# Even mixer of the second block: the convolution's norm ahead of the third pair of heads, its spread in an accumulator bank, and the modulation steps dealt out at other places

## The chip, the cores and the metric

The kernel runs on one core of a Trainium2 chip. The metric is device time in microseconds of one execution. A core has five engines that work from their own instruction streams in order: TensorE (PE, matmuls; its weight loads are PEld), VectorE (DVE), ScalarE (ACT), GpSimd (POOL) and SyncE (SP, which here only issues transfers).

## The reference, cut to what matters

Three transformer blocks follow one another on one sequence of 256 tokens with 1024 channels, in fp32. The change lies in the second block, in the mixer of its first layer:

```python
def even_mixer(hm, w_in, q_g, k_g, conv_w, conv_b, ln_g, ln_b, w_out, rope, kv_prefix):
    proj = hm @ w_in
    q = rms_norm_2(proj[..., :ATTN_WIDTH]..., q_g)         # 8 heads of 64
    k, v = split_kv(proj[..., ...], k_g)                   # 2 kv heads
    q = apply_rope(q, *rope); k = apply_rope(k, *rope)
    k = concatenate([kv_prefix[0], k]); v = ...            # 256 context rows ahead
    attn = block_attention(q, k, v)
    g = u * sigmoid(gate)                                  # 512 channels each
    g = depthwise_conv(g, conv_w) + conv_b                 # 31 taps
    g = silu(layer_norm(g, ln_g, ln_b))
    return concatenate([attn, g]) @ w_out

def second_block(...):
    for i in range(2):
        m = ada_mod(c, ada_w[i], ada_b[i])                 # silu(c) @ w + b, 6 x 1024 numbers
        hn = modulate(rms_norm_2(h, norm1_g[i]), m[0], m[1])
        ...                                                # i = 0: the context with ada_mod(c_ctx), then even_mixer
        h = h + m[2] * mixer(hn)                           # i = 1: short_conv_mixer
        h = h + m[5] * ec_moe(modulate(rms_norm_2(h, norm2_g[i]), m[3], m[4]), ...)
```

`ec_moe` has 16 experts, each of which takes its 32 best tokens; 12 MB of weights belong to each expert. The modulation matrices `ada_w` hold 24 MB for each layer.

## The kernel before

**The mixer's stages.** `even_mixer` (L1107) norms the block's input, projects k and v (`ev_kv`), the queries (`ev_q`), and value and gate of the convolution's first two channel groups (`gated(0)`, `gated(1)`). Then it norms the 256 context rows (transposes `nt` L525; squares' sums, `newton` L357 to L367, `across` L379, which spreads a column of scales over all partitions by a matmul with ones; L563 scales, L571 casts), projects the context's k and v, and takes norm and rotary embedding of the heads (L581 to L1236, with transposes `tr` L598). From there on the source calls `convolve` of four channel groups, `gated(2)`, `gated(3)`, and `attend` of four pairs of heads, and the layer norm over the convolution's channels (L1252 to L1274). Last comes the output projection `ev_out` in `residual` (4 weight slabs, the convolution's half of the channels first), then the router, the choice of tokens, their gathering, and the experts' matmuls (L1387).

**Steps within these.** `gated(g)` (L1142) projects two slabs, gates them (L1154), writes the result to DRAM (`evd`, L1158) and reads it back four times shifted (`sh`, L1162), all on SP. `convolve` is 32 matmuls of 32x256 (L1178). `attend` scores each pair of heads in four matmuls (`fsc`, L651), takes maxima on DVE (L655), exponentials on ACT (L658), reciprocals and products on DVE (L660, L663), transposes on PE (`fpt`, L666), copies on ACT and multiplies with v (`ev_o`, L671). In the norm of the convolution `ev_mean` is L1254, `ev_var` L1264; the spread (L1265, by `across` L386) takes a PSUM bank of `gen`.

**Weights.** A slab of 128x2048 (1 MB) comes by SP into one of the 7 places of the ring `w` (`slab`, L338). `weights` (L400) loads it (L406) and splits each half of it into a rounded part (ACT, L392) and the rest (DVE, L393) in one of three `ws` buffers; `mm3` then has three matmuls (L424 to L426). The modulation's slabs go through the same ring (L1001).

**Modulation.** `Ada.steps` (L985) is a generator. One step is one chunk of 512 outputs: two slabs. Even chunks run on PE: 16 matmuls (L1007), a copy on ACT (L1028), two transposes (L1030). Odd chunks (listed in `VEC`) run on ACT (L1013) and DVE (7 accumulations `ada_acc`, L1015), with four column matmuls at the end (`ada_t`, L1023). In `even_mixer` 14 steps are left, which `k.step(n)` deals out: `weights` asks for .46 of a step after each slab, `gated(g)` for `PACE[1][g]`, the place behind the context's k and v for `PACE[1][4]`, and `k.step(99)` for what is left. So a call of `k.step` sets where in the program the step's loads and instructions stand.

**PSUM.** Banks are `acc` (3), `o` (1) and `gen` (4, taken in turn by scores, transposes, modulation and small results).

**What sets the order.** No order is written by hand. A list scheduler takes the program's order as priority and a time model of its own, and fixes each engine's order of instructions when the program is built; the engines then run their lists in order. A wait in such a list holds all that stands behind it on that engine.

**The experts' weights.** `place` (L1378) asks for expert slabs early, in 21 places (the ring's seven, seven of `more`, the others where buffers come free), and the loads stand in SP's list among the others.

Of the kernel before, what the change touches and what calls it, by code (L numbers as in the profile page):

```python
# [250 lines left out]
HOLD = 8  # L251

FIRST = 10
VEC, PACE = [[1,3,5,7,9,11],[1,3,5,7,9,11]], (.46, (2,2,3,2,4))

RAW = 3

# [27 lines left out]
class Kern:  # L285
# [27 lines left out]
    def t(self, name):  # L313
        return self.tab[name]
# [58 lines left out]
        self.nc.vector.tensor_scalar(x, ss, 1.0 / dim, EPS, op0=OP.mult, op1=OP.add)  # L373
        return self.newton(x, n, pool)

    def across(self, col, pool, name):

        n = col.shape[-1]
        if pool is None:  # L379
            d = self.sm.tile([128, 512], F32, tag="sq", name=name, bufs=1)[:, :128 * n].rearrange("p (n s) -> p n s", n=n)  # L380
        else:
            d = pool.tile([128, n, 128], F32, name=name, bufs=1)
        self.nc.vector.tensor_tensor(d, self.ident[:, None, :].to_broadcast([128, n, 128]),
                                     col[:, :, None].to_broadcast([128, n, 128]), op=OP.mult)
        p = self.gen(name)
        self.spread = self.nc.tensor.matmul(p[:, :128 * n], self.ones, d.rearrange("p n s -> p (n s)"), start=True, stop=True)  # L386
        return p[:, :128 * n]

# [677 lines left out]
def block2(k, ada, ns):  # L1066
    nc, tc = k.nc, k.tc
    with ExitStack() as cx:
        pl = cx.enter_context(tc.tile_pool(name="b2", bufs=1))
        ring = cx.enter_context(tc.tile_pool(name="ring2", bufs=RING_B))  # L1070
        k.rings.append((ring, RING_B))
        k.load_table("t2", pl)
        more = cx.enter_context(tc.tile_pool(name="more", bufs=MORE))
        for l in range(2):
            if l == 0:
                ns, route = even_mixer(k, ada, ns, pl, more)
            else:
                n = len(k.loads)
                ns, route = short_conv(k, ada, ns, pl, srow, last)
            if l == 0:  # L1080
                box = []

                def start(room):
                    gain, shift = ada.gains(1, "norm11", 0)
                    box.append(k.norm_state(gain=gain, shift=shift, fp=Cut([(room[0], 0)], 2), n=4))
                    return lambda c: k.norm_part(box[1], k.x, c, 256)

                def early():
                    box.append(pl.tile([128, D], F32, tag="mrow", name="sc_mrow"))
                    ada.row(1, 2, box[0])  # L1090
                last = moe(k, ada, l, ns, route, pl, more, start, early, None)
                srow, ns = box
            else:
                fin = FinalNorm(k, pl)
                moe(k, ada, l, ns, route, pl, more, fin.start, fin.load, k.loads[n + HOLD])
        k.rings.pop()
        return fin.finish()
# [24 lines left out]
def even_mixer(k, ada, ns, bp, more):  # L1122
    nc, tc, t = k.nc, k.tc, k.t
    with ExitStack() as cx:
# [20 lines left out]
        def gated(g):  # L1145
            box = []

            def evac(i, p):
                if i == 0:
                    box.append(p)  # L1150
                    return
                h = gpool.tile([128, S], name="evh")
                nc.scalar.activation(h, p, AF.Tanh, scale=0.5)
                nc.vector.scalar_tensor_tensor(gp[:, g, 15:15 + S], h, 1.0, box[0], op0=OP.add, op1=OP.mult)  # L1154
            k.columns("ev_ug", g, xs, 8, evac)
            k.step(PACE[1][g])
            d = tc.dram_tile([128, S + 32], F32, name=f"evd{g}")
            nc.sync.dma_start(d, gp[:, g])  # L1158
            sh = shs[g % 2]
            for b in range(4):  # L1160
                src = bass.AP(tensor=d.tensor, offset=d.offset + b, ap=[[S + 32, 32], [32 * (S + 32), 4], [1, S + 28]])
                nc.sync.dma_start(sh[32 * b:32 * b + 32], src)  # L1162
            return sh
# [3 lines left out]
        def diagonals(g):  # L1167
            dg = dgs[g] = dgp.tile([128, 4, 8, 32], name="dg")
            for c in range(4):
                nc.gpsimd.tensor_tensor(dg[:, c], t("ev_half")[:, None, :].to_broadcast([128, 8, 32]),  # L1170
                                        cw[:, 4 * g + c, :, None].to_broadcast([128, 8, 32]), op=OP.mult)

        def convolve(g, sh):
            dg = dgs[g]
            p = k.acc("ev_conv")
            for j in range(8):
                for c in range(4):
                    nc.tensor.matmul(p[32 * c:32 * c + 32, :S], dg[:, c, j], sh[:, c, 4 * j:4 * j + S], start=j == 0, stop=j == 7,  # L1178
                                     tile_position=(0, 32 * c))
            nc.scalar.activation(cv[:, g], p[:, :S], AF.Identity, bias=t("ev_cb")[:, g:g + 1])  # L1180

        def attend(j):
            o = k.bank("o", "ev_o")
            k.full_attention(atp, o[:, :S], qt[:, j], kt_, lambda i, h: v[:, i, 64 * h:64 * h + 64], 4)
            k.split(yh[:, j], yl[:, j], o[:, :S])
# [14 lines left out]
        sh = [gated(0), gated(1)]  # L1200
# [37 lines left out]
        at = cx.enter_context(tc.tile_pool(name="evat", bufs=1))  # L1238
# [1 line left out]
        convolve(0, sh[0])  # L1240
        diagonals(2)
        sh.append(gated(2))
        attend(0)
        convolve(1, sh[1])
        diagonals(3)
        sh.append(gated(3))
        attend(1)
        convolve(2, sh[2])
        attend(2)
        convolve(3, sh[3])  # L1250

        mean = k.acc("ev_mean")  # L1252
        for g in range(4):
# [7 lines left out]
        var = k.acc("ev_var")  # L1261
        for tt in range(2):
            for g in range(4):
                nc.tensor.matmul(var[:, tt:tt + 1], sq[g // 2][:, g % 2, 128 * tt:128 * tt + 128], k.ones[:, 0:1], start=g == 0, stop=g == 3)  # L1264
        rs = k.across(k.rsqrt(var[:, 0:2], 2, 512), at, "ndiag2")  # L1265
        for g in range(4):
            f = sqp.tile([128, 2, S], F32, tag="nf", name="ev_y")
            y, h = f[:, 0], f[:, 1]
            nc.vector.scalar_tensor_tensor(y, cv[:, g], t("ev_lng")[:, g:g + 1], rs, op0=OP.mult, op1=OP.mult)
            nc.vector.tensor_scalar(y, y, t("ev_lnb")[:, g:g + 1], None, op0=OP.add)  # L1270
            nc.scalar.activation(h, y, AF.Tanh, scale=0.5)
            nc.vector.scalar_tensor_tensor(y, h, 1.0, y, op0=OP.add, op1=OP.mult)
            k.split(yh[:, 4 + g], yl[:, 4 + g], y, 0.5)
        attend(3)  # L1274
        k.step(99)
        return k.residual("ev_out", (yh, yl), 8, mrow, sqp, route.half, order=(1, 0)), route
# [755 lines left out]
```

## Time and profile before

| | |
|---|---|
| median of 3 runs | 2212.45 us (2212.28 to 2213.82) |
| profiled execution | 2207.99 us, of which the span is 2206.2 us |
| PE busy | 1827.9 us (83%) |
| DVE, ACT busy | 1056.3 us (48%), 723.5 us (33%) |
| mean granted TensorE clock | 0.889 |
| bytes by DMA | 638.00 MB, 289 GB/s over the span |
| instructions | 35790 |

The profile divides the span into slices, engines and waits. Busy time of PE is modelled: an instruction that runs at the lower clock is longer in it, and a busy PE is not PE at its peak. The profile shows each fp32 matmul of these sizes as two rows (16 matmuls of L1007 are 32 rows; a transpose is one). The granted clock is a share of full speed. Of the whole span, the DMA engines move 417 to 419 GB/s in the stretches of the experts and 96 to 400 in the others.

### The profile page before, as it was taken

What the parts mean: (1) busy time and instruction counts of PE and PEld (TensorE: products, weight loads), DVE (VectorE), ACT (ScalarE), POOL (GpSimd) and SP (SyncE); (2) the same over time, 40 slices, a digit from 0 to 9 for tenths busy, and PEclk for the clock granted to TensorE, in tenths of its full rate; (3) what the DMA queues carried; (4) which work ended last, traced back from release to release, by engine and by line L of the source; (5) the groups of instructions that cost most, each with busy time, mean ns of one, the idle gap of its engine ahead of it and who ended that gap; (6) DMA issues with size and microseconds to landing.
All of it is one profiled execution on the core that took longest, in us unless ns stands there. A gap on an engine that the chain in (4) does not pass through costs nothing.

```text
span 2206.2 us, 35790 instructions
## 1 busy us (share of the span) xinstructions
PE 1827.9 (83%) x14836; PEld 1283.5 (58%) x14836; DVE 1056.3 (48%) x2343; ACT 723.5 (33%) x1363; POOL 47.6 (2%) x90
## 2 busy tenths in 40 slices
PE   7989989898666666789867666667989999999999
PEld 5777877555322222269632222224768998988997
DVE  4885787754100000157500000004877985778984
ACT  4454544342000000035300000003654664555763
POOL 1000010001000000000100000000100000000000
PEclk9999999988877787799987777778999999999999
DMA  9654679938999999997799999999623454434553
GB/s 270 234 198 165 231 298 331 367 132 325 418 419 419 418 418 419 418 416 278 275 418 418 418 419 418 418 419 369 191 96 115 172 192 154 132 136 153 180 177 122
DMA packets 100594, 638.00 MB, mean 289 GB/s; under 512 B 11294, under 2 KB 14238, under 8 KB 28496
## 3 DMA queue, kind: packets, MB, share of 16 engines
q1 hardware_dynamic: 97632, 627.03, 72.7%
q0 software_dynamic: 1360, 4.49, 1.2%
q10 hardware_dynamic: 1440, 4.21, 0.5%
q8 instruction: 116, 1.90, 0.3%
q14 instruction: 46, 0.38, 0.0%
HBM read 632.96 MB, written 2.72 MB: 288 GB/s over the span
## 4 chain that ended last, share of the span: by engine, by line
PE 51%; DMA 38%; DVE 7%; ACT 2%; issue 1%; SPq 0%; ACTq 0%
DMA w<-in_moe_w_down 6%; DMA w<-in_moe_w_up 6%; DMA more<-in_moe_w_up 5%; DMA more<-in_moe_w_down 5%; DMA w<-in_moe_w_gate 4%; PE up L426 4%; PE up L425 3%; PE up L424 3%; DMA more<-in_moe_w_gate 3%; DMA own<-in_moe_w_up 2%; DMA own<-in_moe_w_down 2%; DMA own<-in_moe_w_gate 2%; PE down L425 2%; PE down L426 2%; PE down L424 2%; DVE ws L393 2%
## 5 line engine op out<-in xcount | busy, mean ns | idle before, releaser
L393 DVE TENSOR_TENSOR ws<-w,ws 128x1024 fp32r<-128x1024 f32 (+5 forms) x316 | 376.9, 1195 | 171.6 <-ACT ws L392 169.4
L392 ACT CAST ws<-w 128x1024 fp32r<-128x1024 f32 (+5 forms) x316 | 320.6, 1020 | 271.7 <-PE down L426 63.9
L1486 ACT ACTIVATE hd<-gu 128x256 f32<-128x256 f32 x32 | 12.3, 383 | 717.0 <-PE gu L1387 717.0
L1487 DVE SCALAR_TENSOR_TENSOR hd<-hd,gu 128x256 f32<-128x256 f32 x32 | 13.5, 421 | 479.8 <-ACT hd L1486 479.8
L1387 PE MATMUL gu<-w,xst 128*32 128x256 f32 x1376 | 122.0, 483 | 62.0 <-DMA w<-in_moe_w_gate 34.3
L425 PE MATMUL up<-ff_xh,ws 128*128 128x256 f32 x608 | 171.1, 284 | 2.6 <-DVE ws L393 2.6
L426 PE MATMUL up<-ff_xl,ws 128*128 128x256 f32 x608 | 170.4, 283 | 2.7 <-DVE ff_xl L393 2.7
L424 PE MATMUL up<-ff_xh,ws 128*128 128x256 f32 x608 | 168.2, 283 | 0.1
L1387 PE MATMUL gu<-more,xst 128*32 128x256 f32 x1344 | 111.0, 457 | 65.7 <-DMA more<-in_moe_w_up 43.5
L1387 PEld LDWEIGHTS gu<-w,xst 128*32 128x32 f32 x1376 | 44.0, 130 | 135.0 <-DMA w<-in_moe_w_up 53.8
L1501 DVE SCALAR_TENSOR_TENSOR ysm<-dn,gcol,moe_mq 128x256 f32<-128x256 f32 x30 | 14.5, 484 | 221.0 <-PE dn L1387 221.0
L1387 PEld LDWEIGHTS gu<-more,xst 128*32 128x32 f32 x1344 | 43.2, 125 | 128.9 <-DMA more<-in_moe_w_up 68.8
L425 PEld LDWEIGHTS up<-ff_xh,ws 128*128 128x128 f32 x608 | 115.7, 190 | 3.7 <-DVE ws L393 3.5
L426 PEld LDWEIGHTS up<-ff_xl,ws 128*128 128x128 f32 x608 | 115.3, 190 | 3.1 <-DVE ff_xl L393 3.1
L424 PEld LDWEIGHTS up<-ff_xh,ws 128*128 128x128 f32 x608 | 114.0, 190 | 0.5 <-ACT ff_xh L392 0.5
L1387 PE MATMUL gu<-ws,xst 128*32 128x256 f32 x608 | 56.4, 498 | 24.3 <-DMA ws<-in_moe_w_up 14.1
L1015 DVE SCALAR_TENSOR_TENSOR ada_acc<-w,ada_st,ada_acc 128x512 f32<-128x512 f32 x98 | 73.6, 758 | 4.7 <-ACT ada_acc L1013 4.2
L424 PE MATMUL down<-ws,ff_h 128*128 128x512 f32 x176 | 69.7, 396 | 0.0
L425 PE MATMUL down<-ws,ff_l 128*128 128x512 f32 x176 | 69.5, 395 | 0.0
L1387 PE MATMUL dn<-w,ht 128*32 128x256 f32 x672 | 55.4, 465 | 14.6 <-DMA w<-in_moe_w_down 8.3
L1387 PE MATMUL dn<-more,ht 128*32 128x256 f32 x672 | 55.4, 474 | 12.6 <-DMA more<-in_moe_w_down 8.3
L426 PE MATMUL down<-ws,ff_h 128*128 128x512 f32 x176 | 63.8, 396 | 0.0
(650 smaller groups left out, 4032.5 us busy)
## 6 DMA issues: line engine op xcount, KB each, us to landing
w<-in_wd SPq DMA_DIRECT2D x144, 1024.0 KB, 5.0
w<-in_ada_w SPq DMA_DIRECT2D x48, 1024.0 KB, 5.5
more<-in_moe_w_up SPq DMA_DIRECT2D x48, 1024.0 KB, 19.8
w<-in_moe_w_gate SPq DMA_DIRECT2D x48, 1024.0 KB, 14.1
w<-in_moe_w_down SPq DMA_DIRECT2D x46, 1024.0 KB, 14.3
more<-in_moe_w_down SPq DMA_DIRECT2D x46, 1024.0 KB, 19.9
w<-in_moe_w_up SPq DMA_DIRECT2D x38, 1024.0 KB, 19.9
more<-in_moe_w_gate SPq DMA_DIRECT2D x36, 1024.0 KB, 19.9
```

The source lines that it names most:

```text
L392: self.nc.scalar.copy(hi, src)
L393: self.nc.vector.tensor_tensor(lo, src, hi.bitcast(F32), op=OP.subtract)
L424: mm(out, lh, rh, start=first, stop=False)
L425: mm(out, ll, rh, start=False, stop=False)
L426: mm(out, lh, rl, start=False, stop=last)
L1015: nc.vector.scalar_tensor_tensor(acc[v], w[:, kt], s, acc[v], op0=OP.mult, op1=OP.add)
L1387: nc.tensor.matmul(out[32 * c:32 * c + 32], lhs(kt), w(1024 * kk + 256 * c, 256), start=kt == 0, stop=kt == 7, tile_position=(0, 32 * c))
L1486: nc.scalar.activation(hd, gu[:, 0:256], AF.Tanh, scale=0.5)
L1487: nc.vector.scalar_tensor_tensor(hd, hd, 1.0, gu[:, 0:256], op0=OP.add, op1=OP.mult)
L1501: nc.vector.scalar_tensor_tensor(y, dn[:, :256], gcol[:, e:e + 1], mq, op0=OP.mult, op1=OP.mult)
```

## The change

Two numbers lists and the order of calls in `even_mixer` are changed. `PACE[1]`, the steps that `gated(0)` to `gated(3)` and the place behind the context's k and v ask for, goes from (2,2,3,2,4) to (1,1,1,1,3). `k.step(2)` is called in three new places: behind `convolve(2)`, behind `convolve(3)` and behind `attend(2)`; all 14 steps are dealt when the second of them is done, so the third call and `k.step(99)` find none. `attend(0)` goes behind `gated(3)`, the whole norm of the convolution ahead of `attend(2)`. The norm's spread takes a bank of `acc`.

```diff
-VEC, PACE = [[1,3,5,7,9,11],[1,3,5,7,9,11]], (.46, (2,2,3,2,4))
+VEC, PACE = [[1,3,5,7,9,11],[1,3,5,7,9,11]], (.46, (1,1,1,1,3))
...
-    def across(self, col, pool, name):
+    def across(self, col, pool, name, wide=False):
...
-        p = self.gen(name)
+        p = (self.acc if wide else self.gen)(name)
...
         convolve(0, sh[0])
         diagonals(2)
         sh.append(gated(2))
-        attend(0)
         convolve(1, sh[1])
         diagonals(3)
         sh.append(gated(3))
+        attend(0)
+        convolve(2, sh[2])
+        k.step(2)
         attend(1)
-        convolve(2, sh[2])
-        attend(2)
         convolve(3, sh[3])
+        k.step(2)
 
         mean = k.acc("ev_mean")
...
-        rs = k.across(k.rsqrt(var[:, 0:2], 2, 512), at, "ndiag2")
+        rs = k.across(k.rsqrt(var[:, 0:2], 2, 512), at, "ndiag2", True)
...
             k.split(yh[:, 4 + g], yl[:, 4 + g], y, 0.5)
+        attend(2)
+        k.step(2)
         attend(3)
         k.step(99)
```

Lines from the norm's mean on stand one later in the changed file, from the router on three later.

**PE, from the context's norm to its projection.** `nt` are the transposes of the context rows, `ndiag` the spread of its scales, `ada` and `ada_t` modulation. Before:

```order
L1023 MATMUL ada_t<-ones,ada_acc 128x1 x4
L1337 MATMUL rshift<-wg,ones 128x16 x8
L525 MATMUL nt<-t_70,ev_w 128x128 x16
L1007 MATMUL ada<-w,ada_st 32x256 x16
L1030 MATMUL ada_t<-t_70,ada_ms 128x128 x2
L1023 MATMUL ada_t<-ones,ada_acc 128x1 x4
L386 MATMUL ndiag<-ev_w,ones 128x256
```

After:

```order
L525 MATMUL nt<-t_70,ev_w 128x128 x11
L386 MATMUL ndiag<-ev_w,ones 128x256
L1007 MATMUL ada<-w,ada_st 32x256 x16
L1023 MATMUL ada_t<-ones,ada_acc 128x1 x4
```

The spread stands ahead of the modulation that stood ahead of it, one group of `ada_t` columns is gone from here, and the shifts of the router and five of the transposes stand earlier, among the projections.

**PE, from the last transposes of the queries (`tr`) to the first scores (`fsc`).** `ev_conv` is the convolution. Before:

```order
L598 MATMUL tr<-t_70,ev_w 128x128 x10
L1007 MATMUL ada<-w,ada_st 32x256 x16
L1023 MATMUL ada_t<-ones,ada_acc 128x1 x4
L1007 MATMUL ada<-w,ada_st 32x256 x12
L1030 MATMUL ada_t<-t_70,ada_ms 128x128 x2
L1007 MATMUL ada<-w,ada_st 32x256 x4
L1178 MATMUL ev_conv<-ev_w 32x256 x16
L651 MATMUL fsc<-ev_w 128x512
```

After:

```order
L1007 MATMUL ada<-w,ada_st 32x256 x16
L598 MATMUL tr<-t_70,ev_w 128x128 x8
L1023 MATMUL ada_t<-ones,ada_acc 128x1 x4
L1030 MATMUL ada_t<-t_70,ada_ms 128x128 x2
L651 MATMUL fsc<-ev_w 128x512 x2
```

One modulation step and 16 matmuls of the convolution stand behind the first scores instead of ahead of them, and another step stands ahead of the transposes. Up to the first scores of the program's list, 176 of the 192 matmuls of L1007 stood in it before and 144 now; of L1023 48 of 56 and now 40; of the convolution's 80 and now 64.

**PE, from the scores of the last pairs to the first matmuls of `ev_out`.** Before:

```order
L666 MATMUL fpt<-t_70,ev_w 128x128 x8
L386 MATMUL ndiag_4602<-ndiag_4600,ones 128x256
L671 MATMUL ev_o<-ev_w 64x256
L651 MATMUL fsc<-ev_w 128x512 x2
L671 MATMUL ev_o<-ev_w 64x256 x7
L666 MATMUL fpt<-t_70,ev_w 128x128 x4
L424 MATMUL ev_out_4721<-ws,ev_yh 128x512
```

After:

```order
L386 MATMUL ndiag_4482<-ndiag_4480,ones 128x256
L1023 MATMUL ada_t<-ones,ada_acc 128x1 x4
L666 MATMUL fpt<-t_70,ev_w 128x128 x4
L671 MATMUL ev_o<-ev_w 64x256
L651 MATMUL fsc<-ev_w 128x512
L666 MATMUL fpt<-t_70,ev_w 128x128 x4
L1007 MATMUL ada<-w,ada_st 32x256 x16
L671 MATMUL ev_o<-ev_w 64x256 x7
L424 MATMUL ev_out_4721<-ws,ev_yh 128x512
```

The first `ev_out` matmul stands behind 15 of the 16 score matmuls before, behind 13 now, and the last modulation step on PE stands right ahead of it.

**SP, from the last read of `sh` to the slabs of `ev_out` (`in_wd`).** Before:

```order
L1162 DMA sh<-evd_4341 32x4x284 x4
L1001 DMA w<-in_ada_w 128x2048
L1378 DMA more<-in_moe_w_up 128x2048
L1001 DMA w<-in_ada_w 128x2048
L406 DMA w<-in_wd 128x2048 x2
```

After:

```order
L1162 DMA sh<-evd_4125 32x4x284 x4
L1001 DMA w<-in_ada_w 128x2048
L1381 DMA more<-in_moe_w_up 128x2048
L1001 DMA w<-in_ada_w 128x2048
L1381 DMA more<-in_moe_w_up 128x2048
L1001 DMA w<-in_ada_w 128x2048 x4
L1381 DMA more<-in_moe_w_up 128x2048
L1001 DMA w<-in_ada_w 128x2048
L406 DMA w<-in_wd 128x2048 x3
```

Behind the last `sh` two modulation slabs and one expert slab were ahead of the first slab of `ev_out`; seven and three are now. The places that the slabs of `ev_out` take are those of steps 11 (PE), 12 (DVE) and 13 (PE) in both kernels. Ahead of the write of the third group's `evd` six modulation slabs stand in a row in the new list, two in the old.

## Rows read from the trace of the kernel before

**Rows 1.** Windows: start:end length, busy PE PEld DVE ACT POOL, clock, DMA share, GB/s.

```profile
316.00:355.60 39.60, 39.60 (x277) 30.54 (x275) 26.73 (x47) 17.59 (x29) 0.40 (x1) 0.98 0.77 295
368.00:405.30 37.30, 32.04 (x318) 24.59 (x318) 35.09 (x95) 12.13 (x23) 6.43 (x9) 0.95 0.95 322
415.00:440.00 25.00, 23.92 (x208) 13.16 (x208) 17.77 (x37) 12.62 (x28) 0.00 (x0) 1.00 1.02 407
440.00:457.00 17.00, 14.04 (x34) 6.37 (x36) 8.24 (x29) 5.65 (x14) 0.00 (x0) 0.51 0.52 213
457.00:471.50 14.50, 12.18 (x55) 6.24 (x52) 8.41 (x23) 6.84 (x20) 0.00 (x0) 0.87 0.00 0
471.50:500.20 28.70, 28.70 (x138) 21.63 (x137) 15.63 (x30) 12.32 (x24) 0.00 (x0) 1.00 0.52 202
530.00:1010.00 480.00, 335.85 (x3706) 163.93 (x3705) 75.48 (x158) 44.58 (x102) 0.80 (x14) 0.81 1.01 417
```

**Rows 2.** Timeline (start, length), PE: last of ev_out and first expert matmul.

```profile
499.94 0.40 PE L426 MATMUL ev_out<-ws,ev_yh 128*128 128x512 f32 x1
...
525.30 1.07 PE L1387 MATMUL gu<-w,xst 128*32 128x256 f32 x16
```

**Rows 3.** Timeline of SP there: the last early place and the loads behind.

```profile
519.75 0.33 SPq L1378 DMA_DIRECT2D x<-in_moe_w_down  x1
526.43 9.76 SPq L1378 DMA_DIRECT2D w<-in_moe_w_down  x6
```

**Rows 4.** Timeline of PE from the context's transposes to its projection.

```profile
356.01 1.94 PE L1337 MATMUL rshift<-wg,ones 128*128 128x16 f32 x16
357.80 3.00 PE L525 MATMUL nt<-t,ev_w 128*128 128x128 f32 x16
360.74 2.49 PE L1007 MATMUL ada<-w,ada_st 128*32 128x256 f32 x32
363.78 0.44 PE L1030 MATMUL ada_t<-t,ada_ms 128*128 128x128 f32 x2 [0.56 <-ACT ada_ms L1028]
364.35 1.02 PE L1023 MATMUL ada_t<-ones,ada_acc 128*128 128x1 f32 x8
365.96 0.70 PE L386 MATMUL ndiag<-ev_w,ones 128*128 128x256 f32 x2 [0.58 <-DVE ev_w L383]
367.91 0.38 PE L424 MATMUL ev_kv<-ws,ev_yh 128*128 128x256 f32 x1 [1.25 <-ACT ev_yh L571]
```

**Rows 5.** Line L1015 in 300 to 500 us: duration (min/median/max, ns), starts.

```profile
L1015 DVE SCALAR_TENSOR_TENSOR ada_acc<-w,ada_st,ada_acc x49: 732/748/1112, 299.0 to 440.4; 128x512 f32<-128x512 f32 x49
```

**Rows 6.** Timeline of PE from the last transposes to the first scores.

```profile
405.35 1.06 PE L598 MATMUL tr<-t,ev_w 128*128 128x128 f32 x8 [4.12 <-DVE ev_w L1236]
406.35 3.56 PE L1007 MATMUL ada<-w,ada_st 128*32 128x256 f32 x32
...
413.08 1.91 PE L1178 MATMUL ev_conv<-ev_w 128*32 128x256 f32 x32
414.92 1.12 PE L651 MATMUL fsc<-ev_w 64*128 64x512 f32 x2
```

**Rows 7.** Timeline of PE: a modulation step, last pairs, spread, first ev_out.

```profile
430.75 1.93 PE L1007 MATMUL ada<-w,ada_st 128*32 128x256 f32 x32
...
463.53 1.33 PE L651 MATMUL fsc<-ev_w 64*128 64x512 f32 x2 [2.32 <-ACT ev_w L658]
...
466.55 1.06 PE L386 MATMUL ndiag<-ndiag,ones 128*128 128x256 f32 x2
...
471.53 0.94 PE L424 MATMUL ev_out<-ws,ev_yh 128*128 128x512 f32 x3
```

**Rows 8.** Timeline of SP: the first two and the last slab of ev_out.

```profile
414.33 0.83 SPq L406 DMA_DIRECT2D w<-in_wd  x2
...
431.89 0.33 SPq L406 DMA_DIRECT2D w<-in_wd  x1
```

**Rows 9.** Transfers in 300 to 560 us: count, size, median us to landing.

```profile
w<-in_wd SPq DMA_DIRECT2D x9, 1024.0 KB, 8.8
```

## The prediction, made from these before the changed kernel ran

> **What bounds the kernel now.** I read the windows first. From 530 to 1010 us the DMA engines are busy at a share of 1.01 and move 417 GB/s, while PE is busy 335.85 of 480.00 us [rows 1]: the experts wait for their weights. What was loaded ahead decides nothing there as long as all 21 early places are full when the experts begin, and they are: the last early load is issued at 519.75 us, SP's next ones stand from 526.43 us, when the first expert matmul (525.30 us) has begun to free places [rows 2, 3]. So the experts' stretch starts later or earlier by what the end of the mixer moves, and each us at the end of `ev_out` (499.94 us) is one us of the whole; router, choice and gathering between 500 and 525 us are the same instructions.
>
> Within the mixer I then read windows and PE's timeline together. From 316 to 355 us PE has no gap (39.60 of 39.60 us). From 368 to 405 us DVE is the bound, 35.09 of 37.30 us. From 415 to 440 us PE is filled again at full clock. From 440 to 471.5 us PE waits for the softmaxes: 14.04 of 17.00 us busy at a granted clock of 0.51, then 12.18 of 14.50 us at 0.87. `ev_out` fills 28.70 us [rows 1].
>
> **The change part by part.** The change removes no arithmetic. It moves modulation, convolution and scores against each other; I price each stretch up to the first scores, then what comes back behind them.
>
> *Up to the context's norm.* One modulation step less on PE is 1.93 us [rows 7]. The 8 shifts (16 rows, 1.79 us from 356.01 to 357.80 us) and 5 of the 16 transposes (5/16 of the 2.94 us from 357.80 to 360.74 us, 0.92 us) come in from behind [rows 4]: 2.71 us at the clock of that place, less at the full one of this stretch (0.98, [rows 1]). Some 0 us; bounds -2 and +1.
>
> *The context's norm.* Before, PE passes from its last projection at 355 us to the context's projection at 367.91 us, 12.9 us, through shifts, transposes, a modulation step, its transposes, columns and then the spread, which waits for DVE, and 1.25 us for ACT [rows 4]. DVE's part of the scales is done among the projections in the new list, so the spread follows the transposes directly and the modulation covers the copy and the scaling. In a row on PE: 11 transposes 2.06, spread 0.70, step 2.49, columns 1.02 us, together 6.3 us. That saves 6.6 us; I take **-6.5**. If the scaling on DVE and ACT isn't hidden by the 3.5 us of modulation, half is left: bounds -3 and -8.
>
> *Heads' norm and rotary embedding.* This stretch is DVE's. Accumulations cost 0.748 us each [rows 5]. By the two lists, 13 of them stand between the context's scaling and the last rotary product before, and 7 after: 6 x 0.748 = 4.5 us less, and part of a weight split more. I take **-4**; bounds 0 (PE's 32.04 us takes over, or a wait for a slab) and -8.
>
> *From the last transposes to the scores.* Before, 9.57 us from 405.35 to 414.92 us: transposes 1.06, a modulation step 3.56, columns, another step, convolution 1.91 us [rows 6]. After, a step stands ahead of the transposes, where PE waits 4.12 us for DVE anyway and so hides it; left are the transposes 1.06, columns 1.02, transposes 0.44 us and a copy, some 3 us. **-6.6**; bounds -4 and -8.
>
> The first scores so come 0 + 6.5 + 4 + 6.6 = 17.1 us earlier.
>
> *What comes back.* Behind the first scores stand, by the lists, two PE steps more (2 x (1.93 + 0.44) = 4.7 us), two groups of columns (2 x 1.02 = 2.0 us) and half a `convolve` (1.91 us): 8.6 us of PE, and 14 accumulations more on DVE (14 x 0.748 = 10.5 us). Against that stands what PE loses there now: idle 1.08 + 2.96 + 2.32 = 6.4 us between 415 and 471.5 us, and by the clock 14.04 x 0.49 + 12.18 x 0.13 = 8.5 us, together 14.9 us [rows 1]. `ev_out` also begins after 13 of 16 score matmuls instead of 15, so that the last pair's waits, of which 2.32 us stands in the timeline [rows 7], lie beside it. I expect a third of the 14.9 us back, 5 us, since added steps fall into gaps only where the order puts them. Net **+3.6**; bounds +8.6 with nothing back and 12 back, -3.4. DVE is busy 16.65 of the 31.5 us from 440 to 471.5 us, so 10.5 us have room if they don't stand ahead of a maximum that PE waits for.
>
> *The spread in an accumulator bank.* No instruction is added. The spread stood at 466.55 us, 5.0 us ahead of `ev_out` [rows 7]; `ev_out` takes that bank back only when the last product of the norm has read it, and it needs that product itself. 0 us; at worst a wait of the spread's own 1.06 us.
>
> *Transfers.* All loads stay. Third gate's write to DRAM stands behind six modulation slabs; its reader, the third convolution, stands behind the first pair, so it is covered by that pair. The rest of the program gets small swaps of order, for which I add 2 us to either side.
>
> **The sum**: 0 - 6.5 - 4 - 6.6 + 3.6 = -13.5 us on the profiled execution's 2207.99 us (span 2206.2 and 1.8 around it), 2194.5 us. The median of the runs lies 4.46 us above that execution, so 2199 us.
>
> **Rivals.** *Nothing is gained.* All 8.6 us come back and the 10.5 us of accumulations stand in DVE's list ahead of the maxima: -17.1 + 19.1 = +2.0, 2214 us. For it speaks that in the pairs' stretch it is the softmax that is waited for, and it needs DVE between PE's matmuls. Against it: DVE is half idle there. The Trainium skill (PSUM — Partial Sum Buffer, Engine vs sequencer instructions) calls the queues of VectorE and ScalarE strict FIFO; by that rule an accumulation that waits for its slab holds every maximum behind it, and the sum would be this rival's, while the idle of the rows alone gives the forecast's.
>
> *Slower: `ev_out` waits for its slabs.* Their places are those of the modulation's last steps. Before, the last slab is issued at 431.89 us [rows 8] and lands 8.8 us later [rows 9], 30.8 us ahead of the first `ev_out` matmul (471.53 us) [rows 7]. Now five more modulation slabs and two more expert slabs stand ahead of the first of them on SP, at 417 GB/s some 2.5 us each, 17.6 us, while `ev_out` wants to begin 13.5 us earlier: 30.8 - 17.6 - 13.5 = -0.3 us. From there on each us late is a us lost, and DVE's and ACT's splits of the late slab stand in their lists ahead of the last softmaxes. With the first and the last slab each a full landing late, 2 x 8.8 = 17.6 us, and nothing taken back by then: -17.1 + 8.6 + 17.6 = +9.1, 2221.5 us. Against it: the first three slabs are freed by steps that stand well ahead of `ev_out` in PE's list, and only the fourth, wanted some 20 us into `ev_out`, by the last.
>
> *A smaller gain.* The context's norm gives only 3 us, DVE's stretch nothing: -3 - 6.6 + 3.6 = -6.0, 2206.5 us. For it speaks that DVE's list there has other work than accumulations, and that transfers at a share of 0.95 [rows 1] may set when they run.
>
> *A larger gain.* 12 of 14.9 us come back: -17.1 + 8.6 - 12 = -20.5, 2192 us. The granted clock was 0.51 where PE had gaps (440 to 457 us) and 1.00 where it was filled (415 to 440 us) [rows 1]; with steps in the gaps it could stay at the upper of its levels, 2.4 GHz. The Trainium skill (Perfetto Trace Analysis, Matmul Optimizations) says that the matmul engine scales its power with utilization, so that matmuls should run back to back; the rows agree, and by that rule the sum would be this one, without it the forecast's.
>
> **How the numbers follow.** Forecast 0.52, larger gain 0.08, smaller gain 0.13, nothing 0.14, slower 0.13. A measurement of this kernel can tell about 0.2%, 4.4 us, from no change. Faster by more than that: 0.52 + 0.08 + 0.13 = 0.73; within it 0.14; slower 0.13. The forecast's own bounds: the stretches' bounds are independent, so from 2191 to 2207 us. The range for 8 in 10 takes in smaller gain and no gain, and leaves out the slower case and half of the larger gain: 2190 to 2214 us.
>
> **What would show it.** Right: the context's projection begins some 6 us after the last gate's projection; the first scores at 396 to 400 us; the windows of the last pairs show PE busier at a granted clock over 0.8; `ev_out` begins at 455 to 461 us with no wait for a transfer; the first expert matmul at 510 to 514 us, and all 21 places full there. Wrong: PE idle ahead of scores or transposes with DVE's accumulations in between, `ev_out` waiting for a DMA, or experts that wait for early slabs at their start.

## Result, and the profile after

The changed kernel takes 2201.68 us (median of 12 runs, 2194.72 to 2212.85) against 2213.78 us (12 runs, 2209.20 to 2215.39) of the kernel before on the same chips: ratio 0.995, 95% interval 0.9934 to 0.9967. Forecast were 2199 us and 13.5 us of gain; 12.1 us came. Measured again it took 2204.78 us (9 runs, 2195.28 to 2215.26) against 2212.93 us, ratio 0.996 (0.9939 to 0.9981), which is 8.2 us. The profiled execution took 2199.33 us, its span is 2197.5 us, 8.7 less than before.

First the windows of the changed kernel, cut at its own marks (columns as in [rows 1]: stretch, length, busy PE, PEld, DVE, ACT, POOL, granted clock, DMA share, GB/s).

```profile
316.00:352.90 36.90, 36.90 (x260) 31.08 (x259) 29.74 (x61) 19.36 (x34) 0.40 (x1) 0.97 0.70 261
352.96:357.46 4.50, 4.50 (x55) 3.24 (x54) 4.46 (x11) 3.46 (x8) 0.00 (x0) 1.00 0.88 233
357.46:392.20 34.74, 31.51 (x347) 24.49 (x346) 29.93 (x88) 11.14 (x21) 7.12 (x9) 1.00 0.90 331
394.28:419.00 24.72, 18.98 (x175) 9.65 (x174) 14.64 (x30) 7.84 (x17) 0.00 (x0) 0.86 1.03 366
419.00:440.00 21.00, 18.05 (x148) 10.65 (x146) 15.04 (x41) 9.15 (x24) 0.00 (x0) 1.00 0.94 378
440.00:459.40 19.40, 18.69 (x81) 9.53 (x81) 16.36 (x40) 10.19 (x21) 0.00 (x0) 0.56 0.48 168
459.40:490.60 31.20, 31.20 (x146) 22.63 (x146) 16.80 (x32) 13.01 (x25) 0.00 (x0) 1.00 0.67 259
520.00:1000.00 480.00, 332.70 (x3685) 161.39 (x3678) 72.17 (x153) 44.09 (x100) 0.67 (x12) 0.81 1.01 416
```

The experts' stretch is as it was, all DMA. Ahead of the first scores every stretch is shorter. Behind them PE now loses time in two places: from 394 to 419 us it is idle for 5.7 us at a granted clock of 0.86, and from 440 to 459 us the granted clock is 0.56, nearer to the lower level of 1.2 GHz than to 2.4 GHz.

PE's timeline at the marks of [rows 4, 6, 7] (start, length, instruction, and in brackets the idle time ahead of it and its releaser):

```profile
352.96 1.36 PE L525 MATMUL nt<-t,ev_w 128*128 128x128 f32 x11
354.16 0.60 PE L386 MATMUL ndiag<-ev_w,ones 128*128 128x256 f32 x2
354.69 1.93 PE L1007 MATMUL ada<-w,ada_st 128*32 128x256 f32 x32
356.55 1.05 PE L1023 MATMUL ada_t<-ones,ada_acc 128*128 128x1 f32 x8
357.46 0.48 PE L424 MATMUL ev_kv<-ws,ev_yh 128*128 128x256 f32 x2
...
389.33 1.93 PE L1007 MATMUL ada<-w,ada_st 128*32 128x256 f32 x32
392.20 1.09 PE L598 MATMUL tr<-t,ev_w 128*128 128x128 f32 x8 [0.93 <-DVE ev_w L1236]
393.12 0.95 PE L1023 MATMUL ada_t<-ones,ada_acc 128*128 128x1 f32 x8
393.94 0.41 PE L1030 MATMUL ada_t<-t,ada_ms 128*128 128x128 f32 x2
394.28 1.17 PE L651 MATMUL fsc<-ev_w 64*128 64x512 f32 x4
399.44 1.12 PE L666 MATMUL fpt<-t,ev_w 128*128 128x128 f32 x4 [3.99 <-DVE ev_w L663]
400.75 3.13 PE L1178 MATMUL ev_conv<-ev_w 128*32 128x256 f32 x30 [0.19 <-DMA ev_w<-evd]
...
409.36 1.50 PE L1178 MATMUL ev_conv<-sh,ev_w 128*32 128x256 f32 x22 [1.56 <-DMA sh<-evd]
...
453.68 3.64 PE L1007 MATMUL ada<-w,ada_st 128*32 128x256 f32 x32
457.25 2.22 PE L671 MATMUL ev_o<-ev_w 128*64 128x256 f32 x14
459.40 0.50 PE L424 MATMUL ev_out<-ws,ev_yh 128*128 128x512 f32 x1
```

The context's norm is the row that the prediction drew up: transposes, spread, modulation, columns, projection without a gap. The wait of 4.12 us ahead of the transposes [rows 6] has become 0.93 us, with a modulation step in its place. New is the wait of 3.99 us of the first pair's transposes for the probabilities, and the modulation step ahead of `ev_out` that takes 3.64 us at the lower clock instead of 1.93 us.

Read off the PE timelines of two profiles of each kernel (the first column of each pair is the profile shown, the second one the repetition among the experiments), in us from the span's start; the two rows of last expert matmuls give where that matmul starts:

| mark | before | before, again | after | after, again |
|---|---|---|---|---|
| context's projection | 367.9 | 368.6 | 357.5 | 358.2 |
| last transposes of the queries | 405.4 | 406.0 | 392.2 | 390.4 |
| first scores | 414.9 | 415.6 | 394.3 | 392.5 |
| first `ev_out` matmul | 471.5 | 472.2 | 459.4 | 461.4 |
| end of `ev_out` | 500.3 | 501.1 | 490.7 | 492.7 |
| first expert matmul | 525.3 | 527.1 | 516.5 | 516.3 |
| last expert matmul, first layer | 933.6 | 935.0 | 925.0 | 925.7 |
| last expert matmul, second layer | 1494.8 | 1499.3 | 1491.1 | 1493.3 |
| span | 2206.2 | 2213.5 | 2197.5 | 2199.1 |

Within the mixer two profiles of one kernel agree within 2 us. The experts begin 9.8 us earlier (mean of both). Up to the second layer's last expert 4.9 us of these are given back, in pieces of 1 to 2 us; the third block then takes 706.1 us instead of 712.8 (span less the mark above it, mean of both) and brings 6.7 us that I hadn't forecast.

### The profile page after: what moved, and what is told of

It reads as the page before. It is cut to its first block, busy times and chain, and to the rows that moved or that the text cites. A ratio compares the mean times of both kernels' runs of the same rounds, so it can differ in the third digit from the quotient of the medians.

```text
span 2197.5 us, 35779 instructions
## 1 busy us (share of the span) xinstructions
PE 1816.0 (83%) x14836; PEld 1276.9 (58%) x14836; DVE 1052.6 (48%) x2343; ACT 721.8 (33%) x1363; POOL 47.0 (2%) x90
## 4 chain that ended last, share of the span: by engine, by line
PE 51%; DMA 40%; DVE 5%; ACT 2%; issue 1%; SPq 0%; ACTq 0%; DVEq 0%
DMA more<-in_moe_w_down 6%; DMA w<-in_moe_w_down 4%; DMA more<-in_moe_w_gate 4%; PE up L426 4%; PE up L424 4%; PE up L425 4%; DMA ws<-in_moe_w_up 4%; DMA ws<-in_moe_w_down 3%; DMA more<-in_moe_w_up 3%; DMA w<-in_moe_w_gate 3%; DMA w<-in_moe_w_up 2%; DMA w<-in_wd 2%; PE down L425 2%; PE down L424 2%; PE down L426 2%; DMA xv<-in_moe_w_up 2%
## 5 line engine op out<-in xcount | busy, mean ns | idle before, releaser
L1490 DVE SCALAR_TENSOR_TENSOR hd<-hd,gu 128x256 f32<-128x256 f32 x32 | 13.5, 421 | 491.0 <-ACT hd L1489 491.0
L425 PE MATMUL up<-ff_xh,ws 128*128 128x256 f32 x608 | 168.6, 281 | 0.0
L424 PE MATMUL up<-ff_xh,ws 128*128 128x256 f32 x608 | 165.3, 281 | 1.6 <-ACT ff_xh L392 1.6
L1015 DVE SCALAR_TENSOR_TENSOR ada_acc<-w,ada_st,ada_acc 128x512 f32<-128x512 f32 x98 | 72.9, 750 | 5.8 <-ACT ada_acc L1013 4.1
L425 PE MATMUL down<-ws,ff_l 128*128 128x512 f32 x176 | 69.5, 395 | 0.0
L1390 PE MATMUL dn<-more,ht 128*32 128x256 f32 x672 | 56.2, 476 | 15.9 <-DMA more<-in_moe_w_down 11.3
```

The lines of the kernel that those rows point to most:

```text
L424: mm(out, lh, rh, start=first, stop=False)
L425: mm(out, ll, rh, start=False, stop=False)
L1015: nc.vector.scalar_tensor_tensor(acc[v], w[:, kt], s, acc[v], op0=OP.mult, op1=OP.add)
L1390: nc.tensor.matmul(out[32 * c:32 * c + 32], lhs(kt), w(1024 * kk + 256 * c, 256), start=kt == 0, stop=kt == 7, tile_position=(0, 32 * c))
L1490: nc.vector.scalar_tensor_tensor(hd, hd, 1.0, gu[:, 0:256], op0=OP.add, op1=OP.mult)
```

## Experiments

Medians are of the runs of each kernel; ratios are to runs of the kernel before that were measured beside it (29 to 32 of them, medians 2211.58 to 2212.93 us).

**Order and bank alone.** The changed kernel with the old step numbers:

```diff
-VEC, PACE = ..., (.46, (1,1,1,1,3))
+VEC, PACE = ..., (.46, (2,2,3,2,4))
```

> The changed kernel with the old numbers of steps (2,2,3,2,4): order of heads, convolution and norm, and the bank, are changed alone; the new calls of k.step find nothing left. Theory (the gain comes from dealing the modulation later): up to the first scores as before, context's projection at 366 to 369 us, first scores at 411 to 416 us, and in all 2209 to 2216 us. Rival (the new order gives the gain, since scores, convolution and last pairs cover one another): first scores as before but the first ev_out matmul at 460 to 465 us and 2200 to 2205 us.

Measured: 2210.76 us, ratio 0.9993 (0.9974 to 1.0012): nothing. The theory's time is right, but not its marks: the first scores stand at 422.9 us, 8 us later than before, `ev_out` from 456.4 to 501.3 us.

**Step numbers alone.** The kernel before with the new numbers:

```diff
+VEC, PACE = ..., (.46, (1,1,1,1,3))
...
         convolve(2, sh[2])
+        k.step(2)
         attend(2)
         convolve(3, sh[3])
+        k.step(2)
```

> The kernel before with the new numbers of steps (1,1,1,1,3) and k.step(2) behind the third and the fourth convolution; order of heads and norm and the spread's bank as before. Theory (later dealing is the gain): context's projection at 356 to 359 us, first scores at 393 to 398 us, the tail longer by 8 to 12 us, in all 2200 to 2206 us. Rival (the gain needs the new order): the tail is longer by 18 us or more, 2210 to 2216 us.

Measured: 2213.14 us, ratio 1.0 (0.9985 to 1.0016): nothing either; here the rival was right. The windows from the spread of the block input's norm (its end stands at 315.6 to 316.4 us in these kernels) to the first scores, and from there to the end of `ev_out`, for order alone, then for numbers alone, tell why:

```profile
316.40:422.90 106.50, 98.80 (x879) 72.38 (x877) 78.60 (x188) 39.48 (x72) 6.84 (x10) 0.92 0.89 312
422.90:501.30 78.40, 73.17 (x343) 44.27 (x343) 48.00 (x110) 36.59 (x79) 0.00 (x0) 0.89 0.56 225
```

```profile
315.90:393.20 77.30, 72.92 (x641) 59.86 (x639) 64.50 (x158) 34.87 (x64) 7.70 (x10) 0.99 0.81 296
393.20:498.30 105.10, 91.88 (x582) 54.54 (x582) 64.11 (x141) 41.01 (x88) 0.00 (x0) 0.85 0.72 270
```

Before, the two stretches were 99.3 and 85.4 us; after, they are 78.5 and 96.4. The numbers alone give the front (77.3 us) and pay 19.7 us for it in the tail. The order alone shortens the tail (78.4 us) by 7.0 us, with more of the convolution ahead of the first pair, and pays 7.2 us in the front. With the numbers alone the front gains 22.0 us, so that the mixer ends 2 us earlier (498.3 instead of 500.3 us), of which nothing is left in the whole. Together the front gains 20.8 us and the tail pays 11.0. Part of what the tail pays with the numbers alone is in its DVE timeline: both splits of an `ev_out` slab stand between the maxima and the reciprocals of a pair, and PE waits 5.82 us for them.

```profile
457.36 0.68 DVE L655 TENSOR_REDUCE fmax<-fsc 128x1 f32<-128x512 f32 x1
...
458.56 0.68 DVE L655 TENSOR_REDUCE fmax<-fsc 128x1 f32<-128x512 f32 x1
459.16 2.35 DVE L393 TENSOR_TENSOR ws<-w,ws 128x1024 fp32r<-128x1024 f32 x2
461.43 0.15 DVE L660 RECIPROCAL frec<-fsum 128x1 f32<-128x1 f32 x1
```

**The bank alone taken back.** The changed kernel with

```diff
-        rs = k.across(k.rsqrt(var[:, 0:2], 2, 512), at, "ndiag2", True)
+        rs = k.across(k.rsqrt(var[:, 0:2], 2, 512), at, "ndiag2")
```

> The changed kernel with the spread of the convolution's norm in a gen bank as before. Theory (the bank is worth nothing): spread within 2 us of 445 us, ev_out from 458 to 461 us, 2199 to 2204 us. Rival (the turn of the gen banks held the spread back behind scores): spread at 450 us or later, ev_out 3 us or more later, 2204 to 2208 us.

Measured: 2203.42 us, ratio 0.9957 (0.9941 to 0.9973), the same as the changed kernel (2204.78 us beside it). But not for the expected reason: the spread comes at 442.9 us, `ev_out` begins at 448.2 us, 11 us earlier, and ends at 487.9 us, the experts begin at 511.4 us, 5 us ahead of the changed kernel. What the mixer gains the third block loses: 717.7 us. From the first scores PE's order in the two kernels is the same up to 437 us; there the changed kernel has two more rows of scores, this one transposes of probabilities. The windows of 10 us in the tail, for the changed kernel, then for this one:

```profile
435.00:445.00 10.00, 8.35 (x30) 3.70 (x28) 7.01 (x26) 4.33 (x10) 0.00 (x0) 0.79 0.72 301
445.00:455.00 10.00, 9.32 (x39) 5.23 (x42) 8.86 (x17) 5.93 (x12) 0.00 (x0) 0.50 0.33 110
```

```profile
435.00:445.00 10.00, 6.25 (x41) 3.52 (x38) 9.10 (x31) 5.75 (x12) 0.00 (x0) 1.00 0.75 304
445.00:455.00 10.00, 8.77 (x60) 5.33 (x60) 10.00 (x22) 4.90 (x11) 0.00 (x0) 1.00 0.74 292
```

Here the clock stays at its upper level. From the first scores to the end of `ev_out`, in the kernel before, the changed one and this one:

```profile
414.90:500.30 85.40, 79.03 (x436) 47.57 (x433) 50.25 (x116) 37.43 (x81) 0.00 (x0) 0.88 0.58 230
394.30:490.70 96.40, 87.00 (x547) 52.54 (x547) 62.94 (x140) 40.17 (x86) 0.00 (x0) 0.88 0.78 294
394.20:487.90 93.70, 79.58 (x547) 48.64 (x547) 62.75 (x140) 40.25 (x86) 0.00 (x0) 0.96 0.82 309
```

Busy time by granted clock estimates PE's work at full clock: 76.6 us in the changed kernel and 76.4 in this one, the same. The changed kernel loses 10.4 us by the clock and 9.4 idle, this one 3.2 and 14.1: most of what the higher clock gives is spent in waits.

**The changed kernel again.**

> The changed kernel once more. Theory: 2199 to 2204 us, and again a spread of single runs over 10 us, against 6 us of the kernel before, with the mixer's marks (context's projection 357.5, first scores 394.3, first ev_out matmul 459.4 us) within 2 us of those of the first profile: what differs from run to run then lies behind the mixer. Rival: the marks in the mixer move by 5 us or more from run to run.

Measured: the marks are in the table above, within 2 us; single runs from 2195.28 to 2215.26 us, their median 0.8 us above the theory's range. The theory held for the marks, but the kernel before spread nearly as widely beside it (2207.39 to 2224.32 us), so the spread tells nothing of the change. Where it arises these two profiles don't show either, since their executions took 2199.33 and 2200.93 us.

**The DRAM round trip on ACT's queue.** For the third and fourth gate:

```diff
+            q = nc.scalar if g > 1 else nc.sync
-            nc.sync.dma_start(d, gp[:, g])
+            q.dma_start(d, gp[:, g])
...
-                nc.sync.dma_start(sh[32 * b:32 * b + 32], src)
+                q.dma_start(sh[32 * b:32 * b + 32], src)
```

> The changed kernel with the DRAM round trip of the third and fourth gate (one write, four reads each) issued by ACT's queue instead of SP's. In the changed kernel the chain into the tail runs through this trip (write 391.7, read landed 409.4 us) while modulation slabs stand ahead on SP. Theory (the trip holds the convolution, and the tail with it): third convolution's first matmul 3 to 8 us earlier, ev_out's end 2 to 5 us earlier, 2197 to 2201 us. Rival (softmaxes and PE's own work set the tail): the trip is shorter, ev_out's end within 1.5 us of the changed kernel's 490.7 to 492.7 us, 2201 to 2206 us.

Measured: 2213.74 us, ratio 1.0002 (0.9987 to 1.0017): all of the gain lost, which neither expected. `ev_out` ends at 501.2 us. ACT's timeline with the transfers that it issues, and PE's wait:

```profile
394.97 0.72 ACT L1013 ACTIVATE ada_acc<-w,ada_st 128x512 f32<-128x512 f32 x1
399.20 6.90 ACTq L1163 DMA_DIRECT2D sh<-evd  x4
406.20 0.69 ACT L658 ACTIVATE ev_w<-fsc,fmax 128x512 f32<-128x512 f32 x1 [10.51 <-DMA ev_w<-evd]
```

```profile
408.28 1.97 PE L666 MATMUL fpt<-t,ev_w 128*128 128x128 f32 x8 [11.66 <-DVE ev_w L663]
```

The four reads of the fourth group come out only from 399.20 to 406.10 us, as transfers of the round trip land, and the first pair's exponentials stand behind them in ACT's list. ACT sits idle 10.51 us, and PE waits 11.66 us for the pair's probabilities instead of 3.99. The Trainium skill (PSUM — Partial Sum Buffer, Engine vs sequencer instructions) calls ScalarE's queue strict FIFO; the trace agrees, with 10.51 us.

**One step at the fourth gate, ahead of the first pair in the source, instead of behind the third convolution.**

```diff
-(.46, (1,1,1,1,3))
+(.46, (1,1,1,2,3))
...
         convolve(2, sh[2])
-        k.step(2)
+        k.step(1)
```

> The changed kernel with one step more at the fourth gate, (1,1,1,2,3), and one less behind the third convolution: one step stands ahead of the second pair instead of behind. Theory (modulation that stands early fills the softmax waits of the first pair and takes work from between the last ones): ev_out's end 2 to 4 us earlier, 2198 to 2202 us. Rival (what comes earlier delays the first scores and the convolution by the same): end of ev_out within 1.5 us, 2201 to 2206 us.

Measured: 2216.26 us, ratio 1.002 (1.0006 to 1.0034): slower than before, against both. The first scores come at 393.9 us, but `ev_out` runs from 451.6 to 505.0 us: it begins early and is stretched by scores, a modulation step and waits between its matmuls.

**The last step on PE instead of DVE.**

```diff
-VEC, PACE = [[1,3,5,7,9,11],[1,3,5,7,9,11]], ...
+VEC, PACE = [[1,3,5,7,9,11],[1,3,5,7,9]], ...
```

> The changed kernel with the last modulation step (chunk 11 of layer 1) on PE instead of ACT and DVE: 7 accumulations less on DVE in the tail (5.2 us), 16 matmuls more on PE (1.9 us at full clock). Theory (DVE's accumulations ahead of maxima lengthen the tail): end of ev_out 1 to 4 us earlier, the PE's wait for maxima and exponentials shorter. Rival (PE's own list sets the tail): end of ev_out 1 to 3 us later.

Measured: 2207.86 us, ratio 0.9979 (0.9966 to 0.9993); `ev_out` ends at 497.4 us, 6.7 us later than 490.7 (4.7 than 492.7), beyond the rival's 1 to 3. The theory falls for this step: seven accumulations less on DVE did not shorten the tail. The 16 matmuls more on PE don't explain its length either: from the first scores (394.16 us) to the end of `ev_out` PE is busy 93.07 us at 0.83, an estimated 77.2 us at full clock for 76.6 in the changed kernel, but 15.8 us are lost by the clock instead of 10.4.

**The last four steps left out** (8 slabs less; the results of the four chunks, 8 to 11 of layer 1, are set to zero):

```diff
-chain(ada.steps(0, VEC[0], range(FIRST, 12)), ada.steps(1, VEC[1]))
+chain(ada.steps(0, VEC[0], range(FIRST, 12)), ada.steps(1, VEC[1], range(8)))
```

> The changed kernel without the last four modulation steps (chunks 8 to 11 of layer 1, 8 slabs; their results are set to zero). It prices what the dealing moved into the tail. My sum held that two steps and their accumulations in the tail cost 3.6 us net; the profile of the changed kernel shows about 11 us. Theory (moved work is paid in full in the tail, two PE and two DVE steps without cover): end of ev_out 8 to 14 us earlier than 490.7 us, 2187 to 2195 us. Rival (softmaxes set the tail, steps are covered): end of ev_out 0 to 5 us earlier, 2195 to 2202 us.

Measured: 2187.87 us (4 runs), ratio 0.9873 (0.9848 to 0.9897); `ev_out` ends at 478.6 us, 12.1 us earlier than 490.7, at the theory's price. Four steps in the tail are not covered by waits, so far as one build shows. Their 8 slabs aren't loaded either, so this prices steps and transfers together.

**Repetitions.** The kernel with the gen bank, and the kernel before:

> The changed kernel with the spread in a gen bank, once more. In its first profile the mixer ended 2.8 us earlier than in the changed kernel (ev_out's end 487.9) and the experts of the second layer 7.6 us earlier (1483.5), but the third block took 717.7 us against 706.4. Theory A (the third block's length belongs to the built order): 715 us or more again, ev_out's end within 2 us of 488. Theory B (it varies from run to run with the granted clock): 703 to 713 us, and this run's time moves with it.

> The kernel before, once more. Theory A (marks and third block belong to the build): first scores 414.9, ev_out's end 500.3, first expert matmul 525.3 us within 2 us, third block 710 to 713 us. Theory B (they vary from run to run): one of these off by 4 us or more.

Measured: 2200.11 us (5 runs), ratio 0.9954 (0.9941 to 0.9967), end of `ev_out` at 487.2 us, third block 715.5 us; the kernel before 2213.53 us, third block 714.2 us, 1.2 above the first theory's range. So in two profiles each the third block's length goes mostly with the built order (706.4 and 705.8 us for the changed kernel, 717.7 and 715.5 with the gen bank, 711.4 and 714.2 before). The two executions of the kernel before that were profiled differ by 7.3 us (2207.99 and 2215.27 us), of which 0.8 us stand at the end of `ev_out`: between these two most of the difference arises behind the mixer. One profile speaks against the build: in the kernel with ACT's queue the third block took 703.0 us, in an execution 13 us below its median.

**Neighbouring numbers**, both with the gen bank: one step more behind `attend(2)`, `(1,1,1,1,2)`, and one step earlier at the context's k and v, `(1,1,1,1,4)` with `k.step(1)` behind the third convolution.

> The changed kernel with the gen bank and (1,1,1,1,2): one more step later, behind attend(2). If dealing later pays by itself, the first scores come 1 to 3 us earlier and the whole gains up to 4 us, 2197 to 2202 us. If the tail pays for what is dealt into it, ev_out's end is 3 to 8 us later than 488 and the whole 2204 to 2210 us.

> The changed kernel with the gen bank, (1,1,1,1,4) and one step less behind the third convolution: one step earlier, at the context's k and v. If the tail pays in full for what is dealt into it and the stretch of DVE doesn't notice one step, ev_out's end is 3 to 6 us earlier than 488 and the whole 2195 to 2201 us. If the stretch of DVE grows by the step (first scores 4 us or more later), the whole is 2202 to 2208 us.

Measured: 2208.23 us, ratio 0.999 (0.9978 to 1.0001), `ev_out` ends at 502.3 us, 14 to 15 later than with the same bank; and 2205.56 us, ratio 0.9971 (0.9956 to 0.9986), first scores at 400.8 us, end at 495.8 us. In both the tail, or the stretch of DVE, pays. No version that does all of the work beat the changed kernel by more than these runs can tell.

## Why the prediction held, point by point

**What bounds the kernel** held where it was needed: up to the first expert matmul 131.4 MB have been moved in the kernel before, the changed one and every other one that loads all slabs, so the same early places were full, and the experts moved by the mixer's end (9.8 us for 9.0 us at the end of `ev_out`, means of both profiles). That each us there is one us of the whole failed: 4.9 us were given back behind it. In the first profiles, from the last expert matmul of the first layer to the next layer's first projection 36.7 us pass instead of 33.6; but the kernel before, again, took 36.9 us there, so part of this was the profile that I worked from. What returned the rest isn't settled.

**Up to the context's norm and in it.** I took 0 and -6.5 us; measured are -2.0 us (the last projection of the gates ends before 352.96 instead of 354.98 us) and -8.4 us (4.5 us instead of 12.9 to the context's projection), both at my bounds or 0.4 beyond. The row was right, its price was not: I added durations from rows whose stretch before has a granted clock of 0.83 (357.80 to 367.91 us), 2.06, 2.49 and 1.02 us [rows 4]; with no wait between them the clock is 1.00, and the transposes, the step and the columns pass in 1.20, 1.86 and 0.91 us from start to start.

**Heads' norm and rotary embedding.** -4 us forecast; -2.7 us in the first pair of profiles, -5.2 us in the second. **To the scores.** -6.6 forecast, -7.5 and -7.5 us measured; the wait is used as foreseen. Together the first scores came 20.6 and 23.1 us earlier, not 17.1.

**What comes back** is the term that was mis-sized: +3.6 us forecast, beyond its bound of 8.6 measured: from the first scores to the end of `ev_out` 96.4 instead of 85.4 us, +11.0 us (+14.7 in the second pair). PE's added work was about right: 87.00 us at 0.88 are some 76.6 us of PE at full clock, against 79.03 us at 0.88, 69.5 us, before, 7.1 us for my 8.6. DVE's was not: 28 accumulations start behind the first scores instead of 10, 18 more and not 14, which at 0.748 us are 13.5 us instead of 10.5. Wrong above all was that a third of the 14.9 us that PE loses there would come back. It loses 96.4 - 76.6 = 19.8 us, before 85.4 - 69.5 = 15.9, so that nothing came back and 3.9 us more went. Two places say where. From 394 to 419 us the first pair waits 3.99 us for its own softmax; the convolution behind it waits for its round trip through DRAM, which lands just ahead of 400.75 us and again of 409.36 us; and DVE's list puts accumulations between maxima and products:

```profile
395.54 0.68 DVE L655 TENSOR_REDUCE fmax<-fsc 128x1 f32<-128x512 f32 x1
396.14 0.74 DVE L1015 SCALAR_TENSOR_TENSOR ada_acc<-w,ada_st,ada_acc 128x512 f32<-128x512 f32 x1
396.80 0.68 DVE L655 TENSOR_REDUCE fmax<-fsc 128x1 f32<-128x512 f32 x1
397.40 0.74 DVE L1015 SCALAR_TENSOR_TENSOR ada_acc<-w,ada_st,ada_acc 128x512 f32<-128x512 f32 x1
...
398.91 0.47 DVE L663 TENSOR_SCALAR ev_w<-ev_w,frec 128x512 f32<-128x512 f32 x1
```

And from 440 to 459 us the clock falls again, 0.56: 18.69 x 0.44 = 8.2 us, as much as before [rows 1] (0.65 from 440.00 to 461.44 us in the second profile). Accumulations among the maxima are the first rival's mechanism, beside the forecast's front; the tail paid 11.0 of that rival's 19.1 us. How much of it the accumulations cost is not shown: three of them lie within the wait of 3.99 us, 0.66 us each from start to start, and with seven fewer of them in the last step the tail didn't get shorter. None had idle time ahead of it here, so none held a maximum by waiting for its slab. With four steps left out, 12.1 us came back, which fits a tail that had no room.

**The spread's bank** I took at 0 us. On the whole it is 0 (2203.42 and 2204.78 us side by side), but by two amounts that cancel: the mixer ends 3 to 5 us later with it, the third block is some 10 us shorter. The third block's code is untouched. That the scheduler's order makes the difference is argued from two profiles of each build and not shown; why it differs stays open.

**Transfers.** `ev_out` didn't wait for a slab; its first three were issued from 431.35 us and the last at 454.00 us. The slower rival's place showed up elsewhere: with the numbers alone, in the splits on DVE shown above.

**The small swaps** behind the mixer I put at 2 us to either side; they were +4.9 us up to the second layer's experts and -6.7 us in the third block. In the page's groups the feed-forward's projection `up` in the last block shows the latter, first the kernel before, then the changed one (busy us, mean ns | idle ahead):

```profile
L425 PE MATMUL up<-ff_xh,ws 128*128 128x256 f32 x608 | 171.1, 284 | 2.6 <-DVE ws L393 2.6
L426 PE MATMUL up<-ff_xl,ws 128*128 128x256 f32 x608 | 170.4, 283 | 2.7 <-DVE ff_xl L393 2.7
L424 PE MATMUL up<-ff_xh,ws 128*128 128x256 f32 x608 | 168.2, 283 | 0.1
```

```profile
L425 PE MATMUL up<-ff_xh,ws 128*128 128x256 f32 x608 | 168.6, 281 | 0.0
L426 PE MATMUL up<-ff_xl,ws 128*128 128x256 f32 x608 | 168.4, 281 | 0.0
L424 PE MATMUL up<-ff_xh,ws 128*128 128x256 f32 x608 | 165.3, 281 | 1.6 <-ACT ff_xh L392 1.6
```

7.4 us less busy and 3.8 us less idle, at a clock of 1.00 instead of 0.98 between 1700 and 1800 us. So that the total came out near the forecast is in part luck, since three errors cancel. By the means of both pairs of profiles the front gave 21.9 us, 4.8 more than its 17.1, the tail took 12.9 us, 9.3 more than its 3.6, and what I took for noise behind the mixer gave 2.6 us: together 11.6 instead of 13.5 us.

**The clock.** I cited the Trainium skill (Perfetto Trace Analysis, Matmul Optimizations), that the matmul engine scales its power with utilization, for the larger gain. The steps in the gaps didn't bring it: 0.56 stands where 0.51 stood. In the kernel with the gen bank it was 1.00 through that stretch, with as little work ahead of it (8.35 x 0.79 = 6.6 us at full clock from 435 to 445 us in the changed kernel, 6.25 us there). From 445 to 455 us both profiles of the kernel before and both of the changed kernel show 0.50, both with the gen bank 1.00, so it goes with the build in these three. These rows don't tell what decided it.

**The signs that I named.** `ev_out` began about where I said (459.4 and 461.4 us for 455 to 461) and waited for no transfer. The context's projection came 4.5 us behind the last gate's instead of some 6. The first scores came earlier than 396 us, the clock in the last pairs stayed below 0.8, and the first expert matmul came at 516.5 and 516.3 us instead of 510 to 514. One sign of being wrong stood in the trace: PE idle ahead of transposes with DVE's accumulations in between. The mechanism of the front was right, that of the tail was not.

## What to carry to other kernels

Work that is moved out of one stretch is paid in another; price the receiving stretch by leaving that work out, not by the idle time that a profile shows there, since here the idle time inside a chain of softmaxes took no work in. Where two changes share a stretch, try each alone: here later dealing without the new order, and the new order without later dealing, were both worth nothing, and together 0.4 to 0.5%. Where a scheduler fixes the order, a local change can move the time of code far away, and here two profiles of one build agreed on that part within 3 us: compare marks inside the program, and two builds, before a few us are laid to the change.

## What the runs showed of the hardware beyond expectation

A transfer that ACT issues and that has to wait for another holds ACT's arithmetic: 6.90 us of issuing, ACT idle 10.51 us ahead of an exponential, PE idle 11.66 us instead of 3.99. Single runs of one build differ by up to 20 us (2195.28 to 2215.26 us), while its marks in the mixer agree within 2 us in the two executions that were profiled. One profile can mislead on the total: that of the kernel with ACT's queue took 2200.86 us, the lowest of its 12 runs, whose median is 2213.74 us, though its `ev_out` ended as late as before. And from 445 to 455 us PE had a granted clock of 0.50 in one build and 1.00 in another, in two profiles of each, though the work from the first scores to the end of `ev_out` is the same in both (some 76.6 and 76.4 us at full clock).
